# Two of the seven half-size products of each FFN chunk issued as 512-column passes over an operand's high and low parts

## The chip, the cores and the metric

One core of one Trainium2 chip. The metric is the device time of one execution in microseconds (us). Before the change it was 820.54 us, the median of 3 runs (820.32 to 820.89). All other times below come from one profiled execution.

## The reference

One encoder layer on 512 positions of width 1024: a feed-forward network (FFN), a mixer (Fourier part and attention), a second FFN, a last norm.

```
def swiglu(h, w_gate, w_up, w_down):
    return (jax.nn.silu(h @ w_gate) * (h @ w_up)) @ w_down
...
        x = x + 0.5 * swiglu(rms_norm(x, ffn1_norm), ffn1_w_gate, ffn1_w_up, ffn1_w_down)
        ...
        x = x + 0.5 * swiglu(rms_norm(x, ffn2_norm), ffn2_w_gate, ffn2_w_up, ffn2_w_down)
    return rms_norm(x, final_norm)
```

`w_gate` and `w_up` are 1024 x 2752, `w_down` is 2752 x 1024. The 2752 hidden units are 21 chunks of 128 and a tail of 64. The change is in how the gate and up products of most chunks are made, in both FFNs.

## The kernel before

**Precision.** [...] ScalarE (ACT) makes a high part with a copy that rounds, VectorE (DVE) the low part with a subtraction (`lows`, L127 and L128).

**Seven products.** With the positions in two halves of 256 and the depth in two halves of 512, the gate and up products of a chunk are one 2 x 2 block product. It is done by seven products in place of eight (a Strassen-Winograd scheme). The operand's seven combinations are made once per FFN by `operands` (L333) and kept as high and low parts in the tile `rt`: `[P, 7, 2, KH, HALF]`, that is combination, high or low, depth block (KH = 4), 256 positions. The weights' combinations are made for every chunk by `prepare` (L366): the DMAs of the raw weights are issued by SP, DVE adds and subtracts (`combine`, L394), ACT rounds (L379, L388), DVE subtracts (L128), and the parts lie in slots of the tile `ring`. The products are named by their weights: a11, a12, s1, s2, s4, s3, a22.

**One chunk.** `seven` (L407) runs over the chunks of a group. For a chunk, `multiply` (L413) writes a product as 12 passes of 256 columns (4 depth blocks by 3 passes) into half of a 512-column PSUM bank. `step` (L431) gives their order and what reads the banks:

| step | product | bank | then |
|---|---|---|---|
| 0 | a11 | r, opened | ACT copies r to p1 (L428) |
| 1 | a12 | p2, opened | DVE: g right half = p2 + p1 (L441) |
| 9 of the chunk ahead | a22 | its r | ACT copies r to u right half (L464), DVE u = g * u, ACT and DVE split it into `at` |
| 3 | s1 | q, opened | ACT copies q to p5 (L428) |
| 4 | s2 | r, added to | ACT copies r to u2 (L428) |
| 5 | s4 | q, added to | DVE: g left half = q + u2 (L451), ACT silu over g (L452) |
| 6 | s3 | r, added to | ACT copies r to u left half (L456), DVE adds p5 (L457) |

A product that adds to a bank can start only when the copy of what the bank held is done: s4 waits for the copy to p5, s2 for that to p1, s3 for that to u2. Pieces of `prepare` for the next chunk stand between the steps.

**Groups.** After the chunks of a group `down` (L485) makes the eight 128-row blocks of the down product for that group: 512-column passes (L184, tile `dn`) that read `at` and weights in `ring`. The operands of a 512-column pass are read and written in the order 4 x 32 x 4 (`turned`, L177), and what they read as operand begins four elements into its tile (NEAR, and FRONT + LOWER, L28, L116 and L292); `rt` has no such shift. In all 35 chunks go through `seven` (17 in the first FFN, 18 in the second, 5 or 6 in each group). At the start of each group one 256-column pass is cut in 64 and 192 columns (CUT, L41 and L160).

**Order.** PE and SP run in the order of the code (L121). For ACT, DVE and GpSimd (POOL) the tile framework's scheduler sets the order when the program is built, so a change of one instruction can move others on these engines.

Of the kernel before, what the change touches and what calls it, by code (L numbers as in the profile page):

```python
# [6 lines left out]
F32 = mybir.dt.float32  # L7
F32R = mybir.dt.float32r
# [24 lines left out]
GROUPS2 = ((0, "t", 1), range(2, 8), range(8, 14), range(14, 21))  # L33
PLACES = 7
HALF = S // 2
USES = "a11", "a12", "s1", "s2", "s4", "s3", "a22"
PIECES = (0, 2, 2, 0, 2, 1, 1)
KH = KD // 2
# [48 lines left out]
def encoder(ctx, tc, A, out):  # L87
# [19 lines left out]
    def bank(name):  # L107
        return pp.tile([P, S], F32, tag="bank", name=name)
# [173 lines left out]
    def ffn(norm, after, wgu, wd, wdt, groups, opening, closing):  # L282
# [6 lines left out]
        with tc.tile_pool(name=f"act{n_}", bufs=1) as ap, tc.tile_pool(name=f"sums{n_}", bufs=2) as sp:  # L289
            room(ap, 128)  # L290
            acts = ap.tile([P, PLACES * 2 * S + ROOM], F32R, name=f"at{n_}")
            at = acts[:, FRONT + LOWER : FRONT + LOWER + PLACES * 2 * S].rearrange("p (n a b) -> p n a b", a=2, b=S)  # L292
            rt = ap.tile([P, 7, 2, KH, HALF], F32R, name=f"rt{n_}")
            wt, raws = [], {}
            free, where = list(range(PLACES)), {}

# [36 lines left out]
            def operands(rp, i0, i1):  # L333
                for i in range(i0, i1):
# [72 lines left out]
            def seven(js, done):  # L407
# [4 lines left out]

                def multiply(ps, wn, on, w, first):  # L413

                    (whi, wlo), (mhi, mlo) = w[wn], (part[on][:, i] for i in range(2))
                    for i in range(KH):
                        ks = slice(i * P, (i + 1) * P)
                        for o, (a, b) in enumerate(((whi, mhi), (whi, mlo), (wlo, mhi))):
                            for t in parts_of(next(count)):
                                nc.tensor.matmul(  # L420
                                    ps[:, t], a[:, ks], b[:, i, t], start=first and i == 0 and o == 0,
                                    stop=i == KH - 1 and o == 2, skip_group_check=not first,
                                )
                    give(*w.get((wn, "slots"), ()))

                def kept(ps, n, j):
                    t = sp.tile([P, HALF], F32, tag=n, name=f"{n}{n_}_{j}")
                    nc.scalar.copy(t, ps)  # L428
                    return t

                def step(j, w, n):  # L431
                    b = banks.setdefault(j, {})
                    if n == 0:
                        b["r"] = bank(f"r{n_}_{j}")[:, :HALF]
                        multiply(b["r"], "a11", "b11", w, True)
                        b["p1"] = kept(b["r"], "p1", j)
                    elif n == 1:
                        ps = bank(f"p2{n_}_{j}")[:, :HALF]
                        multiply(ps, "a12", "b21", w, True)
                        b["g"] = tp.tile([P, S], F32, tag="g", name=f"g{n_}_{j}")  # L440
                        nc.vector.tensor_tensor(out=b["g"][:, HALF:], in0=ps, in1=b["p1"], op=ALU.add)  # L441
                    elif n == 3:
                        b["q"] = bank(f"q{n_}_{j}")[:, :HALF]
                        multiply(b["q"], "s1", "t1", w, True)
                        b["p5"] = kept(b["q"], "p5", j)
                    elif n == 4:
                        multiply(b["r"], "s2", "t2", w, False)
                        b["u2"] = kept(b["r"], "u2", j)
                    elif n == 5:
                        multiply(b["q"], "s4", "b22", w, False)  # L450
                        nc.vector.tensor_tensor(out=b["g"][:, :HALF], in0=b["q"], in1=b["u2"], op=ALU.add)  # L451
                        nc.scalar.activation(b["g"], b["g"], AF.Silu)  # L452
                    elif n == 6:
                        multiply(b["r"], "s3", "t3", w, False)
                        b["u"] = tp.tile([P, S], F32, tag="u", name=f"u{n_}_{j}")
                        nc.scalar.copy(b["u"][:, :HALF], b["r"])  # L456
                        nc.vector.tensor_tensor(  # L457
                            out=b["u"][:, :HALF], in0=b["u"][:, :HALF], in1=b["p5"], op=ALU.add
                        )
                    elif n == 9:  # L460
                        multiply(b["r"], "a22", "t4", w, False)
                        u, i = b["u"], place(j)
                        h, l = at[:, i, 0], at[:, i, 1]
                        nc.scalar.copy(u[:, HALF:], b["r"])  # L464
# [1071 lines left out]
```

## Time and profile before

| | |
|---|---|
| median of 3 runs | 820.54 us |
| the profiled execution, whole | 820.94 us |
| its span, first to last instruction | 818.9 us |
| PE busy | 812.4 us (99%), 5362 matmuls |
| DVE busy | 637.5 us (78%), 1003 instructions |
| ACT busy | 483.1 us (59%), 810 instructions |
| DMA | 89.97 MB, mean 110 GB/s |
| granted TensorE clock | full in all 40 slices |

A matmul's duration in the profile is that of one pass from start to end (276 ns for 256 columns, 380 for 512). Passes overlap, so what a pass costs on PE is the distance from its start to the next pass's start. It is read from two rows of the timeline: the difference of their starts, divided by the passes between them. The same holds for DVE, whose instructions overlap a little.

### The profile page before, as it was taken

To read this page: it belongs to the slowest core of one execution; us is meant where nothing else is said; L and a number is where in the kernel's file an instruction comes from. 1 tells how busy PE (TensorE), PEld (TensorE's weight loads), DVE (VectorE), ACT (ScalarE), POOL (GpSimd) and SP (SyncE) were. 2 spreads that over 40 slices of the span, in tenths; PEclk is the share of its full clock that TensorE was granted. 3 is DMA by queue.
4 is the path that set the end of the run, shared out by engine and by line. 5 is a ranking of instruction groups with operands and counts; after the bars stand their busy time and mean duration, and the time that the engine had idled before them with its cause. 6 is when DMAs were issued, how large, how long until landed. Compare 5 with 4: busy or idle time off the path is not lost.

```text
span 818.9 us, 13611 instructions
## 1 busy us (share of the span) xinstructions
PE 812.4 (99%) x5362; PEld 746.1 (91%) x5362; DVE 637.5 (78%) x1003; ACT 483.1 (59%) x810; POOL 29.3 (4%) x31
## 2 busy tenths in 40 slices
PE   9999999999999999999999999999999999999997
PEld 7889999899989998889998888899989999899987
DVE  7898896479856847799998578999945896479574
ACT  7763674257523735699998448456632673257462
POOL 0110000000000000221000001100000000000001
PEclk9999999999999999999999999999999999999999
DMA  7664322333141223342101234542232322322222
GB/s 258 174 145 179 124 93 77 124 104 142 59 151 71 90 70 116 129 147 66 65 26 52 77 112 127 123 176 108 94 122 114 127 100 69 132 104 97 69 78 103
DMA packets 31568, 89.97 MB, mean 110 GB/s; under 512 B 3728, under 2 KB 9232, under 8 KB 31504
## 3 DMA queue, kind: packets, MB, share of 16 engines
q1 hardware_dynamic: 27776, 82.61, 29.1%
q0 software_dynamic: 3008, 5.51, 3.7%
q10 hardware_dynamic: 720, 0.98, 0.3%
q8 instruction: 42, 0.69, 0.3%
q14 instruction: 22, 0.18, 0.1%
HBM read 84.24 MB, written 2.10 MB: 105 GB/s over the span
## 4 chain that ended last, share of the span: by engine, by line
PE 95%; DVE 2%; ACT 1%; POOL 1%; issue 1%; DMA 0%; POOLq 0%; DVEq 0%; ACTq 0%
PE dn L184 25%; PE r L420 23%; PE q L420 12%; PE gu L184 8%; PE mix L184 6%; PE p L420 6%; PE gu L709 3%; PE mix L1203 2%; PE mix L1169 2%; PE mix L1007 1%; PE mix L1008 1%; PE mix L1009 1%; PE mix L1066 1%; PE mix L1143 1%; PE mix L1144 1%
## 5 line engine op out<-in xcount | busy, mean ns | idle before, releaser
L420 PE MATMUL r<-rt,ring 128*128 128x256 f32 x1686 | 209.2, 276 | 0.0
L184 PE MATMUL dn<-at,ring 128*128 128x512 f32 x900 | 202.5, 380 | 0.0
L420 PEld LDWEIGHTS r<-rt,ring 128*128 128x128 f32 x1686 | 200.3, 188 | 0.8
L184 PEld LDWEIGHTS dn<-at,ring 128*128 128x128 f32 x900 | 168.0, 188 | 28.3
L420 PE MATMUL q<-rt,ring 128*128 128x256 f32 x840 | 106.6, 276 | 0.0
L128 DVE TENSOR_TENSOR ring<-s,ring 128x1024 fp32r<-128x1024 f32 x70 | 85.5, 1221 | 23.8 <-ACT ring L379 20.8
L420 PEld LDWEIGHTS q<-rt,ring 128*128 128x128 f32 x840 | 100.4, 188 | 0.0
L544 DVE SCALAR_TENSOR_TENSOR gx<-dn,gx 128x512 f32<-128x512 f32 x61 | 41.9, 688 | 67.1 <-PE dn L184 67.1
L379 ACT CAST ring<-s 128x1024 fp32r<-128x1024 f32 x70 | 73.5, 1050 | 28.3 <-PE p L420 13.7
L170 ACT CAST ring<-raw_dn 128x768 fp32r<-128x768 f32 (+3 forms) x58 | 45.3, 784 | 72.8 <-PE dn L184 61.9
L128 DVE TENSOR_TENSOR ring<-raw_dn,ring 128x768 fp32r<-128x768 f32 (+3 forms) x58 | 51.5, 892 | 5.7 <-PE r L420 4.4
L420 PE MATMUL p<-rt,ring 128*128 128x256 f32 x420 | 53.3, 276 | 0.0
L128 DVE TENSOR_TENSOR ring<-raw_g,ring 128x1024 fp32r<-128x1024 f32 x35 | 42.7, 1220 | 11.7 <-PE p L420 10.2
L420 PEld LDWEIGHTS p<-rt,ring 128*128 128x128 f32 x420 | 50.2, 188 | 0.0
L184 PE MATMUL gu<-ring 128*128 128x512 f32 x216 | 48.9, 381 | 0.0
L379 ACT CAST ring<-raw_g 128x1024 fp32r<-128x1024 f32 x35 | 36.8, 1051 | 17.2 <-DMA raw_g<-in_wgu 11.5
L184 PEld LDWEIGHTS gu<-ring 128*128 128x128 f32 x216 | 40.4, 188 | 6.9
L428 ACT COPY p<-r 128x256 f32<-128x256 f32 x35 | 12.9, 369 | 44.9 <-PE r L420 44.6
L452 ACT ACTIVATE g<-g 128x512 f32<-128x512 f32 x35 | 22.2, 633 | 23.9 <-DVE g L451 23.6
L388 ACT CAST ring<-raw_u 128x512 fp32r<-128x512 f32 x35 | 21.8, 624 | 16.0 <-PE q L420 15.7
L184 PE MATMUL mix<-near,ring 128*128 128x512 f32 x120 | 28.8, 381 | 0.0
L465 DVE TENSOR_TENSOR u<-g,u 128x512 f32<-128x512 f32 x35 | 24.0, 687 | 6.1 <-ACT u L464 6.0
(266 smaller groups left out, 1314.3 us busy)
## 6 DMA issues: line engine op xcount, KB each, us to landing
raw_g<-in_wgu SPq DMA_DIRECT2D x35, 512.0 KB, 3.8
raw_u<-in_wgu SPq DMA_DIRECT2D x35, 512.0 KB, 4.3
raw_dn<-in_wd SPq DMA_DIRECT2D x40, 384.0 KB, 3.1
raw_gu<-in_wgu SPq DMA_DIRECT2D x12, 512.0 KB, 3.7
raw_o<-in_wo SPq DMA_DIRECT2D x8, 512.0 KB, 3.5
raw_dn<-in_wd SPq DMA_DIRECT2D x8, 448.0 KB, 3.7
raw_wq<-in_wins SPq DMA_DIRECT2D x4, 512.0 KB, 3.5
raw_f<-in_winf SPq DMA_DIRECT2D x4, 512.0 KB, 3.5
```

The lines of the kernel that those rows point to most:

```text
L128: nc.vector.tensor_tensor(out=lo, in0=src, in1=asf(hi), op=ALU.subtract)
L170: nc.scalar.copy(hi[:, :n, :], raw[:, :n, :])
L184: nc.tensor.matmul(ps, a, b, start=first and b is mhi and a is whi, stop=last and a is wlo)
L379: nc.scalar.copy(hi, src)
L388: nc.scalar.copy(hi, src)
L420: nc.tensor.matmul(ps[:, t], a[:, ks], b[:, i, t], start=first and i == 0 and o == 0, stop=i == KH - 1 and o == 2, skip_group_check=not first,
L452: nc.scalar.activation(b["g"], b["g"], AF.Silu)
L465: nc.vector.tensor_tensor(out=u, in0=b["g"], in1=u, op=ALU.mult)
L544: nc.vector.scalar_tensor_tensor(out=x[d][:, t], in0=ps[:, t], scalar=0.5, in1=x[d][:, t], op0=ALU.mult, op1=ALU.add)
L709: nc.tensor.matmul(turned(pss[c]), w[:, k % 2, c], turned(m[k]), start=k == 0 and m is hh and w is hi, stop=k == KD - 1 and w is lo,)
L1169: nc.tensor.transpose(pts[n][:, c * P : (c + 1) * P], prob[t, b, c][:, kc * P : (kc + 1) * P], ident)
L1203: nc.tensor.matmul(turned(outs[t, b]), w, turned(p), start=kc == 0 and i == 0, stop=kc == 3 and i == 1)
```

## The change

`rt` becomes `[P, 7, KH, 2, HALF]`, so that for a depth block the 256 high columns and the 256 low ones lie side by side. The products a12 and s4 (`WIDE`) are then made of eight passes and not twelve: four passes of 512 columns, high weights by high and low operand at once, which leave two sums in the two halves of the bank, and after them four passes of 256 columns, low weights by high operand, into the left half. DVE adds the two halves: where it added one half and a tile (L441, L451), it now adds one half and the tile, and then the other half. The other five products keep their twelve passes in their order. a12 and s4 are those whose bank DVE reads; the other five, read by ACT, go through the same helpers as before.

```
-            rt = ap.tile([P, 7, 2, KH, HALF], F32R, name=f"rt{n_}")
+            rt = ap.tile([P, 7, KH, 2, HALF], F32R, name=f"rt{n_}")
...
-                        h, l = rt[:, c, 0, i], rt[:, c, 1, i]
+                        h, l = rt[:, c, i, 0], rt[:, c, i, 1]
...
-                    (whi, wlo), (mhi, mlo) = w[wn], (part[on][:, i] for i in range(2))
+                    whi, wlo = w[wn]
                     for i in range(KH):
-                        ks = slice(i * P, (i + 1) * P)
-                        for o, (a, b) in enumerate(((whi, mhi), (whi, mlo), (wlo, mhi))):
-                            for t in parts_of(next(count)):
-                                nc.tensor.matmul(
-                                    ps[:, t], a[:, ks], b[:, i, t], start=first and i == 0 and o == 0,
-                                    stop=i == KH - 1 and o == 2, skip_group_check=not first,
-                                )
+                        ks, m = slice(i * P, (i + 1) * P), part[on][:, i].rearrange("p a b -> p (a b)")
+                        start, stop = first and i == 0, i == KH - 1
+                        if wn in WIDE:
+                            nc.tensor.matmul(turned(ps), whi[:, ks], turned(m), start=start, stop=False, skip_group_check=True)
...
+                    if wn in WIDE:
+                        for i in range(KH):
+                            ks, m = slice(i * P, (i + 1) * P), part[on][:, i, 0]
+                            nc.tensor.matmul(
+                                ps[:, :HALF], wlo[:, ks], m, start=False, stop=i == KH - 1, skip_group_check=True
+                            )
...
+                def added(out, ps, other, n):
+                    nc.vector.tensor_tensor(out=out, in0=ps[:, :HALF], in1=other, op=ALU.add)
+                    if n in WIDE:
+                        nc.vector.tensor_tensor(out=out, in0=ps[:, HALF:], in1=out, op=ALU.add)
...
-                        nc.vector.tensor_tensor(out=b["g"][:, HALF:], in0=ps, in1=b["p1"], op=ALU.add)
+                        added(b["g"][:, HALF:], ps, b["p1"], "a12")
...
-                        nc.vector.tensor_tensor(out=b["g"][:, :HALF], in0=b["q"], in1=b["u2"], op=ALU.add)
+                        added(b["g"][:, :HALF], b["q"], b["u2"], "s4")
```

PE has 5070 matmuls in the program in place of 5350, DVE 70 additions more. SP and POOL keep their order. What moves is shown at three places.

PE, in the chunk 8 of the first FFN, before; `r_8`, `p_8` and `q_8` are the banks of this chunk, `r_7` that of the chunk ahead.

```order
L420 MATMUL r_8_1185<-rt_129,ring 128x256 x12
L420 MATMUL p_8_1200<-rt_129,ring 128x256 x12
L420 MATMUL r_7_1063<-rt_129,ring 128x256 x12
L420 MATMUL q_8_1237<-rt_129,ring 128x256 x12
L420 MATMUL r_8_1185<-rt_129,ring 128x256 x12
```

These are a11, a12, a22 of the chunk ahead, s1 and s2, twelve passes each.

The same place on PE with the change, from the last passes of a11 to the first of a22; the passes with high weights stand at L425 and those with low weights at L430.

```order
L425 MATMUL r_8_1161<-rt_129,ring 128x256 x2
L430 MATMUL r_8_1161<-rt_129,ring 128x256
L421 MATMUL p_8_1176<-rt_129,ring 128x4x32x4 x4
L436 MATMUL p_8_1176<-rt_129,ring 128x256 x4
L425 MATMUL r_7_1045<-rt_129,ring 128x256 x2
L430 MATMUL r_7_1045<-rt_129,ring 128x256
```

The twelve passes into `p_8` are four of 512 columns and four of 256, and PE goes from 256 columns to 512 and back at each such product.

DVE, at the end of the first run of `seven` in the first FFN, before: chunk 9 is the last of that run, `raw_dn_0_1` the down weights that PE needs first behind it, `s_0_10` and `raw_g_10` belong to the first chunk of the next group.

```order
L128 TENSOR_TENSOR ring<-raw_g_10_1468,ring 128x1024
L441 TENSOR_TENSOR g_9_1329<-p_9_1316,p_9_1314 128x256
L394 TENSOR_TENSOR s_0_10_1473<-raw_g_10_1468,s_0_10_1472 128x512
L128 TENSOR_TENSOR ring<-s_0_10_1472,ring 128x1024
L465 TENSOR_TENSOR u_8_1296<-g_8_1213,u_8_1296 128x512
L128 TENSOR_TENSOR ring<-raw_u_10_1469,ring 128x512
L128 TENSOR_TENSOR ring<-raw_dn_0_1_1406,ring 128x768
L451 TENSOR_TENSOR g_9_1329<-q_9_1347,u_9_1374 128x256
L128 TENSOR_TENSOR at_128<-u_8_1296,at_128 128x512
```

The low part of the down weights stands behind one addition of this chunk (L441).

The same place on DVE with the change, where L442 is the first addition of a wide product and L444 the second.

```order
L129 TENSOR_TENSOR ring<-raw_g_10_1432,ring 128x1024
L442 TENSOR_TENSOR g_9_1295<-p_9_1286,p_9_1272 128x256
L395 TENSOR_TENSOR s_0_10_1437<-raw_g_10_1432,raw_u_10_1433 128x512
L395 TENSOR_TENSOR s_0_10_1437<-raw_g_10_1432,s_0_10_1436 128x512
L493 TENSOR_TENSOR u_8_1266<-g_8_1185,u_8_1266 128x512
L129 TENSOR_TENSOR ring<-s_0_10_1436,ring 128x1024
L444 TENSOR_TENSOR g_9_1295<-p_9_1286,g_9_1295 128x256
L129 TENSOR_TENSOR ring<-raw_u_10_1433,ring 128x512
L129 TENSOR_TENSOR ring<-raw_dn_0_1_1370,ring 128x768
L442 TENSOR_TENSOR g_9_1295<-q_9_1314,u_9_1341 128x256
L129 TENSOR_TENSOR at_128<-u_8_1266,at_128 128x512
```

The low part of the down weights now stands behind the second addition of chunk 9 too, and behind both second additions of chunk 8.

ACT, in the chunks 8 and 9, before: L452 is the silu of a chunk, `p_8` with `q_8` the copy to p5 for which s4 waits, `u_8` with `r_8` the copies out of the bank r.

```order
L428 COPY p_8_1250<-q_8_1237 128x256
L428 COPY u_8_1264<-r_8_1185 128x256
L379 CAST ring<-s_0_9_1184 128x1024
L466 CAST at_128<-u_7_1174 128x512
L452 ACTIVATE g_8_1213<-g_8_1213 128x512
L456 COPY u_8_1296<-r_8_1185 128x256
L379 CAST ring<-raw_g_10_1468 128x1024
L428 COPY p_9_1314<-r_9_1301 128x256
L379 CAST ring<-s_0_10_1472 128x1024
L464 COPY u_8_1296<-r_8_1185 128x256
```

The silu stands ahead of three copies and casts of the same chunk.

The same place on ACT with the change, where L476 is the silu and L447 all copies but that of step 6 (L486).

```order
L447 COPY p_8_1211<-q_8_1210 128x256
L447 COPY u_8_1237<-r_8_1161 128x256
L380 CAST ring<-s_0_9_1160 128x1024
L494 CAST at_128<-u_7_1150 128x512
L486 COPY u_8_1266<-r_8_1161 128x256
L380 CAST ring<-raw_g_10_1432 128x1024
L447 COPY p_9_1272<-r_9_1271 128x256
L476 ACTIVATE g_8_1185<-g_8_1185 128x512
L447 COPY u_8_1266<-r_8_1161 128x256
L380 CAST ring<-s_0_10_1436 128x1024
```

The silu, which now waits for the second addition, has moved behind three instructions, into the next chunk, closer to the copies that come after it there; it does so in most chunks.

More of the change, by code (lines that the diff above doesn't have):

```diff
@@ L35 @@
 HALF = S // 2
+WIDE = ('a12', 's4')
 USES = "a11", "a12", "s1", "s2", "s4", "s3", "a22"
@@ L424, in multiply @@
-                    give(*w.get((wn, "slots"), ()))
[L426 to L429, printed above, removed]
+                        ks, m = slice(i * P, (i + 1) * P), part[on][:, i].rearrange("p a b -> p (a b)")
+                        start, stop = first and i == 0, i == KH - 1
+                        if wn in WIDE:
+                            nc.tensor.matmul(turned(ps), whi[:, ks], turned(m), start=start, stop=False, skip_group_check=True)
+                        else:
+                            for o in range(2):
+                                for t in parts_of(next(count)):
+                                    nc.tensor.matmul(
+                                        ps[:, t], whi[:, ks], m[:, o * HALF :][:, t], start=start and o == 0, stop=False,
+                                        skip_group_check=True,
+                                    )
```

39 lines of the change are left out of this document (28 added, 11 removed).

## The prediction

> **What bounds the kernel now.** I read the page's busy times and chain first, then busy time by stretch, then the timeline of one chunk.
>
> ```profile
> PE 812.4 (99%) x5362; PEld 746.1 (91%) x5362; DVE 637.5 (78%) x1003; ACT 483.1 (59%) x810; POOL 29.3 (4%) x31
> PE 95%; DVE 2%; ACT 1%; POOL 1%; issue 1%; DMA 0%; POOLq 0%; DVEq 0%; ACTq 0%
> PE dn L184 25%; PE r L420 23%; PE q L420 12%; PE gu L184 8%; PE mix L184 6%; PE p L420 6%; PE gu L709 3%; PE mix L1203 2%; PE mix L1169 2%; PE mix L1007 1%; PE mix L1008 1%; PE mix L1009 1%; PE mix L1066 1%; PE mix L1143 1%; PE mix L1144 1%
> ```
>
> PE is 95% of the chain that ends last, and 41% of the span is L420, the line that changes. A nanosecond less of PE there is a nanosecond less in all, as long as nothing else comes last. The two stretches of seven products that follow, one ordinary and one with the busiest VectorE, show who could (us; then PE, PEld, DVE, ACT and POOL busy).
>
> ```profile
> 74.00:130.00 56.00, 56.00 (x495) 56.00 (x494) 49.85 (x73) 35.50 (x63) 0.00 (x0) 1.00 0.29 101
> 538.20:594.00 55.80, 55.80 (x494) 55.80 (x493) 52.69 (x79) 35.27 (x62) 0.00 (x0) 1.00 0.31 112
> ```
>
> PE has no gap in either, at the full granted clock (1.00). VectorE is busy 89% and 94% of the time: the change hands work to the second busiest engine.
>
> **The passes.** The end of a run of `seven` on PE, each row starting where its engine gets to it:
>
> ```profile
> 121.73 1.52 PE L420 MATMUL p<-rt,ring 128*128 128x256 f32 x12
> 123.09 1.52 PE L420 MATMUL r<-rt,ring 128*128 128x256 f32 x12
> ...
> 127.17 1.52 PE L420 MATMUL q<-rt,ring 128*128 128x256 f32 x12
> ...
> 129.89 4.12 PE L184 MATMUL dn<-at,ring 128*128 128x512 f32 x18
> 133.85 1.53 PE L420 MATMUL r<-rt,ring 128*128 128x256 f32 x12
> 135.21 27.88 PE L184 MATMUL dn<-at,ring 128*128 128x512 f32 x126
> ```
>
> Twelve 256-column passes take 123.09 - 121.73 = 1.36 us, 113.3 ns each. Eighteen 512-column passes take 133.85 - 129.89 = 3.96 us, 220 ns each. So one wide pass is 2 x 113.3 - 220 = 6.7 ns cheaper than the two it replaces. A wide product is 4 x 220 + 4 x 113.3 = 1333 ns where it was 1360: **26.7 ns less**. Two products in 35 chunks are 70 of them: **-1.87 us**. That is the whole gain that the trace has to give: no row that I read shows a 512-column pass cheaper than 220 ns. The 220 are taken from the `dn` passes because they write and read in the same 4 x 32 x 4 order as the new ones, and there are many of them:
>
> ```profile
> L420 PE MATMUL r<-rt,ring 128*128 128x256 f32 x1686 | 209.2, 276 | 0.0
> L184 PE MATMUL dn<-at,ring 128*128 128x512 f32 x900 | 202.5, 380 | 0.0
> ```
>
> Busy time over count is 225 ns for the second row (with the ends of its stretches), so they all run so.
>
> The Trainium skill, "PSUM — Partial Sum Buffer", Specifications (TRN2), speaks against this order: it says that any access pattern that isn't contiguous slows matmuls significantly. By it the wide passes would cost more than two halves. The `dn` rows don't bear that out: 220 ns for 512 columns in the broken order is less per column than 113.3 for 256 contiguous ones. The skill's "TensorE: Matmul & The Clock Gate", Back-to-back issue gap, gives N / 2.4 + 2.5 ns for a pass; by that fixed part a wide product would save 4 x 2.5 = 10 ns, in all 0.7 us. The rows say 6.7 ns of fixed part, and the measurement decides.
>
> **Changing widths.** Before, PE goes from 256 columns to 512 and back once or twice a group; now at every wide product. Each first pass behind such a change, from the groups of short windows around 133.85 and 135.21 (mean ns is the last but one number):
>
> ```profile
> L420 PE MATMUL r<-rt,ring 128*128 128x256 f32 x1 | 0.3, 279 | 0.0
> ...
> L184 PE MATMUL dn<-at,ring 128*128 128x512 f32 x1 | 0.4, 384 | 0.0
> ```
>
> They are 3 and 4 ns longer than the means of their groups above (276 and 380). I take these: 7 ns x 70 = **+0.49 us**. The bounds: nothing, and what the mixer's 256-column passes show behind a 512-column one:
>
> ```profile
> 410.10 0.38 PE L1144 MATMUL mix<-ks,near 128*128 128x512 f32 x1
> 410.32 0.28 PE L1007 MATMUL mix<-ring 128*128 128x256 f32 x1
> ...
> 411.26 0.28 PE L1009 MATMUL mix<-ring 128*128 128x256 f32 x1
> ...
> 412.62 0.28 PE L1009 MATMUL mix<-ring 128*128 128x256 f32 x1
> ```
>
> From 410.32 to 411.26 are 8 passes at 117.5 ns, from 411.26 to 412.62 are 12 at 113.3. A stream needs some passes to fall into step, here at 8 x 4.2 = 34 ns, which for 70 products would be 2.4 us. I stay with 7 ns, since those rows read the operands `rt` and `at` themselves.
>
> **VectorE's 70 additions.** Three rows of VectorE near the end of the same run:
>
> ```profile
> 115.57 0.42 DVE L441 TENSOR_TENSOR g<-p,p 128x256 f32<-128x256 f32 x1
> 115.90 1.22 DVE L128 TENSOR_TENSOR ring<-raw_g,ring 128x1024 fp32r<-128x1024 f32 x1
> ...
> 128.00 0.95 DVE L128 TENSOR_TENSOR ring<-raw_dn,ring 128x768 fp32r<-128x768 f32 x1
> ```
>
> An addition of this form moves the next start by 0.33 us. A run of 6 chunks gets 12 more, 4.0 us: 53.9 of 55.7 us in the ordinary stretch, where PE's own work hides them; 56.7 of 55.5 in the busiest, where about 1.2 us has to go on behind its end. PE feels lateness only where a result has little time in hand. The nearest is the low part of the first down weights: done at 128.95, and needed by the third `dn` pass at 129.89 + 2 x 0.22 = 130.33, 1.38 us in hand. Ahead of it VectorE now makes three second additions more in chunks 8 and 9 (1.0 us), and PE arrives 12 x 0.027 = 0.3 us earlier: 0.1 us is left. The second place is ScalarE's copy of q to p5, on which s4 waits:
>
> ```profile
> 126.47 0.36 ACT L428 COPY p<-q 128x256 f32<-128x256 f32 x1
> ```
>
> It ends at 126.83 and s4 starts at 127.17: 0.34 us in hand, and much the same in each chunk. ScalarE stands in line behind VectorE at the silu, which now needs the second addition:
>
> ```profile
> ACT g L452 <- DVE g L451: 23.6, 17, 1.9
> ```
>
> It waited there 23.6 us in 17 of 35 chunks, up to 1.9 us. The scheduler has put the silu (0.5 us from start to start) some instructions later, closer to the next chunk's copies; ScalarE's idle time (37% in these stretches) is the cover, but in a chunk where it has none, the copy to p5 is late by some tenths and s4, and all of PE behind it, with it. I take 0.1 us in each of some five places: **+0.5 us**. The bounds are nothing (every lateness hidden) and 3 us: 1.2 us for the busiest stretch, and 0.3 us in each of the six runs.
>
> **What costs nothing.** `rt` is as large as before, its parts are written by instructions of the same shapes while the first group's PE work covers them, and SP and POOL keep their order. The low part is needed one pass earlier in a wide product, but `rt` is complete long before. The seven-product banks are no more than before, 3 a chunk.
>
> **The sum.** -1.87 + 0.49 + 0.5 = -0.88 us. The profiled execution took 820.94 (span 818.9 and 2.0 around it), so 820.06; the median of the runs is 0.4 below that execution, so **819.7 us**.
>
> **Rivals.**
> 1. *All is hidden.* No cost at the changes of width, no waiting: 820.54 - 1.87 = 818.7. For it: the 12 x 113.3 that follow 18 x 512 at 133.85 still take 1.36 us in all. Against it: the 0.34 us in hand. 0.2.
> 2. *The wide passes run in a slower step* (slower than before). A stream of 512-column passes has a second gait:
>
> ```profile
> 331.30 5.44 PE L184 MATMUL mix<-ring 128*128 128x512 f32 x24
> 336.58 0.60 PE L1286 MATMUL mix<-ident,acc 128*128 128x128 f32 x4
> ...
> 338.70 5.14 PE L184 MATMUL mix<-ring 128*128 128x512 f32 x21
> 343.68 0.60 PE L943 MATMUL mix<-ident,kw 128*128 128x128 f32 x4
> ```
>
> 24 passes in 5.28 us are 220 ns; 21 passes of the same line and tiles, behind some small matmuls, in 4.98 us are 237 ns. What a pass reads while the next weights come in seems to matter, and here `rt` lies otherwise to the weights than the operands of any 512-column pass so far (front part: no shift of four elements). At 237 ns the 280 wide passes cost 280 x 17 = 4.76 us more: 819.66 + 4.76 = 824.4. It decides from 226.7 ns on, where the wide pass gains nothing; with the other terms the kernel is over 0.2% slower from about 229. Against it: 900 `dn` passes at 220. The skill's rule on patterns that aren't contiguous points the same way. 0.2.
> 3. *VectorE falls behind.* The additions come late, silu and p5 with them, and s4 waits in most chunks: +3 us in place of +0.5, 822.2, half of it just inside no change and half outside. For it: 94% busy in one stretch. Against it: most of VectorE's results have more in hand. The low part of `raw_g` above ends at 117.12; the next chunk's a11, for which it is made, begins 12 passes into this row, at 120.37:
>
> ```profile
> 119.01 2.88 PE L420 MATMUL r<-rt,ring 128*128 128x256 f32 x24
> ```
>
> That is over 3 us, more than the 1.2 us by which VectorE is late. 0.15.
>
> That the change doesn't do what it says is excluded by the order: 280 passes are gone.
>
> **Chances.** 0.2% is 1.64 us, about what a measurement of this kernel can tell from no change. My forecast has 0.45 and lies inside it, as does half of rival 3: same 0.52. Rival 1 ends at -1.87, just outside: faster 0.2. Rival 2 and the other half of 3: slower 0.28. The range goes from rival 1 to rival 2, 818.6 to 824.4. The likeliest case alone is 819 to 820.6.
>
> **What will show it.** In the profile after: L421 with 280 passes of 512 columns, and from the start of the four to the start of L436's first 0.88 us (rival 2: 0.92 and more); L436's four to the next product's start 0.453 us; a run of twelve behind them still 1.36. Rows of idle PE before L421 `q` with the copy of q as releaser would be the third term, and before the third `dn` pass of a group the down weights. VectorE should be busy some 23 to 29 us more in all. I am wrong if wide passes need over 224 ns, or if PE shows waits of over 1 us in a run of `seven`.

## The result, and the profile after

The changed kernel took 827.31 us (median of 4 runs, 827.14 to 827.76) beside 820.71 for the kernel before (4 runs, 820.32 to 821.59): a ratio of 1.0078, 95% interval 1.0066 to 1.009. It is slower by 6.6 us, where 819.7 was predicted; the time lies outside the range. The profiled execution took 827.76 us with a span of 824.7.

From the page of the changed kernel: busy time, the chain by engine and by line, and the groups of the seven products. The columns behind the bar are busy us, mean ns of one, and idle time ahead.

```profile
PE 818.1 (99%) x5082; PEld 741.1 (90%) x5082; DVE 661.4 (80%) x1073; ACT 483.9 (59%) x810; POOL 29.3 (4%) x31
...
PE 92%; DVE 4%; ACT 1%; DMA 1%; issue 1%; POOL 0%; POOLq 0%; DVEq 0%; ACTq 0%; SPq 0%
PE dn L185 25%; PE r L425 16%; PE mix L185 8%; PE r L430 8%; PE q L425 4%; PE p L421 4%; PE q L421 4%; PE gu L185 4%; PE gu L737 3%; PE q L430 2%; PE p L436 2%; PE q L436 2%; PE mix L1231 2%; PE mix L1197 2%; PE mix L1035 1%; PE mix L1036 1%
...
L425 PE MATMUL r<-rt,ring 128*128 128x256 f32 x1126 | 199.8, 278 | 0.0
...
L430 PE MATMUL r<-rt,ring 128*128 128x256 f32 x560 | 156.0, 279 | 0.0
...
L421 PE MATMUL p<-rt,ring 128*128 128x512 f32 x140 | 37.5, 388 | 0.0
L421 PE MATMUL q<-rt,ring 128*128 128x512 f32 x140 | 37.3, 386 | 0.0
```

The 280 wide passes are there. PE, the engine of the matmuls (TensorE), has 280 of them less, and it is busy 5.7 us *more* (818.1 against 812.4). Two signs point at PE's own pace: the wide passes' means are 388 and 386 ns where the `dn` passes have 380, and the narrow passes, which the change leaves as they were, have risen from 276 to 278 and 279. (A narrow pass has 256 columns, a wide one 512; a narrow product has, for each depth block, two passes with high weights and one with low, a wide one first its four wide passes and then four narrow ones with low weights.)

Where PE waited, in the whole profile after (us in total, times, longest):

```profile
PE busy L682 <- PEq L1547: 0.8, 1, 0.8
PE gu L737 <- ACT ring L723: 0.3, 1, 0.3
```

Both lie at the kernel's start. One more wait, in the seven products, is not in this list, since the records of PE's passes overlap it. It stands in a single chunk of the third run:

```profile
288.01 0.38 ACT L447 COPY p<-q 128x256 f32<-128x256 f32 x1
288.20 0.28 PE L430 MATMUL r<-rt,ring 128*128 128x256 f32 x1
...
288.45 1.18 PE L421 MATMUL q<-rt,ring 128*128 128x512 f32 x4
...
289.47 0.63 PE L436 MATMUL q<-rt,ring 128*128 128x256 f32 x4
```

s4 begins 0.06 us after the end of ScalarE's copy of q to p5 (288.39), 0.25 us behind the start of the last pass of s2, where 0.12 is usual. s2 and s4 take 0.25 us too long between them. In the other 34 chunks that copy ends 0.26 us or more before s4 starts, and PE does not wait. Busy time in the two stretches of before (the first lasts 0.6 us longer now; us, then PE, PEld, DVE, ACT, POOL):

```profile
74.00:130.60 56.60, 56.60 (x443) 54.76 (x443) 52.88 (x84) 35.76 (x63) 0.00 (x0) 1.00 0.30 97
538.20:594.00 55.80, 55.80 (x430) 53.72 (x429) 54.53 (x88) 34.34 (x59) 0.00 (x0) 1.00 0.36 123
```

VectorE is busy 93% and 98% of these, the granted clock is 1.00, PE has no gap. So it is the passes themselves that take longer. One chunk and what follows it, on PE; a row is a group of like passes with its start, and the difference of two starts is what PE needed:

```profile
92.98 1.07 PE L421 MATMUL p<-rt,ring 128*128 128x512 f32 x4
93.89 0.63 PE L436 MATMUL p<-rt,ring 128*128 128x256 f32 x4
94.36 0.40 PE L425 MATMUL r<-rt,ring 128*128 128x256 f32 x2
...
95.77 0.40 PE L425 MATMUL q<-rt,ring 128*128 128x256 f32 x2
...
97.18 0.40 PE L425 MATMUL r<-rt,ring 128*128 128x256 f32 x2
...
98.59 1.06 PE L421 MATMUL q<-rt,ring 128*128 128x512 f32 x4
99.50 0.63 PE L436 MATMUL q<-rt,ring 128*128 128x256 f32 x4
99.96 0.39 PE L425 MATMUL r<-rt,ring 128*128 128x256 f32 x2
...
102.68 0.39 PE L421 MATMUL p<-rt,ring 128*128 128x512 f32 x1
```

Read it from the top. a12's four wide passes take 93.89 - 92.98 = 0.91 us, its four low ones 0.47. Then come a22, s1 and s2, twelve narrow passes each, which the change did not touch: 95.77 - 94.36 = 1.41, 1.41 and 1.41 us. Then s4, 0.91 and 0.46, and behind it s3 and a11 together 102.68 - 99.96 = 2.72, that is 1.36 each as before. **The narrow passes have two paces**, 1.36 / 12 = 113.3 ns (below: the quick step) and 1.413 / 12 = 117.8 ns (the slow step), and at each wide product PE goes over from one to the other.

From the start times of all passes in the trace, per product, from its first pass to the first of what follows (mean of 35, us):

| | a11 | a12 | a22 | s1 | s2 | s4 | s3 | sum of all 35 chunks |
|---|---|---|---|---|---|---|---|---|
| before | 1.382 | 1.360 | 1.361 | 1.360 | 1.360 | 1.360 | 1.360 | 334.0 |
| after | 1.382 | 1.379 | 1.405 | 1.413 | 1.417 | 1.371 | 1.360 | 340.5 |

(a11 holds the cut pass at the head of each of the six runs.) The sum is 6.5 us longer: this is the whole loss, and 0.25 us of it is the wait above (in s2 and s4). Below, "the sum" is this one; what lies outside it took 484.2 us after, 484.9 before, and 484 to 487 in all profiles here, so the sum tells more than one execution's time.

A longer block of wide passes elsewhere does no such thing. The end of the same group, where 18 `dn` passes stand between a11 and the last a22:

```profile
130.44 4.12 PE L185 MATMUL dn<-at,ring 128*128 128x512 f32 x18
134.41 0.39 PE L425 MATMUL r<-rt,ring 128*128 128x256 f32 x2
...
135.77 4.56 PE L185 MATMUL dn<-at,ring 128*128 128x512 f32 x20
```

18 passes in 3.97 us are 220 ns, and the product behind them takes 1.36.

### The profile page after: what moved, and what is told of

It is laid out like the page before. It is cut to its first block, busy times and chain, and to the rows that moved or that the text cites. A ratio compares the mean times of both kernels' runs of the same rounds, so it can differ in the third digit from the quotient of the medians.

```text
span 824.7 us, 13090 instructions
## 1 busy us (share of the span) xinstructions
PE 818.1 (99%) x5082; PEld 741.1 (90%) x5082; DVE 661.4 (80%) x1073; ACT 483.9 (59%) x810; POOL 29.3 (4%) x31
## 4 chain that ended last, share of the span: by engine, by line
PE 92%; DVE 4%; ACT 1%; DMA 1%; issue 1%; POOL 0%; POOLq 0%; DVEq 0%; ACTq 0%; SPq 0%
PE dn L185 25%; PE r L425 16%; PE mix L185 8%; PE r L430 8%; PE q L425 4%; PE p L421 4%; PE q L421 4%; PE gu L185 4%; PE gu L737 3%; PE q L430 2%; PE p L436 2%; PE q L436 2%; PE mix L1231 2%; PE mix L1197 2%; PE mix L1035 1%; PE mix L1036 1%
## 5 line engine op out<-in xcount | busy, mean ns | idle before, releaser
L425 PE MATMUL r<-rt,ring 128*128 128x256 f32 x1126 | 199.8, 278 | 0.0
L425 PEld LDWEIGHTS r<-rt,ring 128*128 128x128 f32 x1126 | 172.2, 189 | 0.8
L430 PE MATMUL r<-rt,ring 128*128 128x256 f32 x560 | 156.0, 279 | 0.0
L430 PEld LDWEIGHTS r<-rt,ring 128*128 128x128 f32 x560 | 105.1, 188 | 0.0
L425 PE MATMUL q<-rt,ring 128*128 128x256 f32 x280 | 51.0, 281 | 0.0
L447 ACT COPY u<-r 128x256 f32<-128x256 f32 x70 | 26.1, 373 | 38.2 <-PE r L430 37.3
L425 PEld LDWEIGHTS q<-rt,ring 128*128 128x128 f32 x280 | 43.2, 190 | 0.0
L447 ACT COPY p<-r 128x256 f32<-128x256 f32 x35 | 12.9, 368 | 46.6 <-PE r L430 45.9
L430 PE MATMUL q<-rt,ring 128*128 128x256 f32 x140 | 39.3, 281 | 0.0
L421 PE MATMUL p<-rt,ring 128*128 128x512 f32 x140 | 37.5, 388 | 0.0
L421 PE MATMUL q<-rt,ring 128*128 128x512 f32 x140 | 37.3, 386 | 0.0
```

The lines of the kernel that those rows point to most:

```text
L421: nc.tensor.matmul(turned(ps), whi[:, ks], turned(m), start=start, stop=False, skip_group_check=True)
L425: nc.tensor.matmul(ps[:, t], whi[:, ks], m[:, o * HALF :][:, t], start=start and o == 0, stop=False, skip_group_check=True,)
L430: nc.tensor.matmul(ps[:, :HALF], wlo[:, ks], m[:, :HALF], start=False, stop=stop, skip_group_check=True)
L447: nc.scalar.copy(out, ps[:, HALF:] if wide else ps[:, :HALF])
```

## The experiments

The theories, as they are named in the expectations. **G**: each wide product switches the step of all later passes, from quick to slow or back. **P**: certain products are slow for their own operands or places. **V**: VectorE's second additions (or what waits for them) are the cost. **L**: the new layout of `rt` and the helpers cost something by themselves. All kernels start from the changed one. "Before" beside them was 821.04 us for 1 to 4, 821.21 for 5, 7, 8 and 9, 821.25 for 6, 10, 14 and 15, and 821.01 for 11, 12 and 13.

**1. No wide product.**

```
-WIDE = ('a12', 's4')
+WIDE = ()
```

> The changed kernel with no product made wide: the new layout of rt, the new helpers, twelve 256-column passes per product again. Theory G (the gait of PE's passes: a wide product leaves the stream of 256-column passes in a slower step, 117.7 ns in place of 113.3, until the next wide product): no wide product, so all products at 1.36 us and the time of before, 820.7. Rival L (the new layout of rt is what makes 256-column passes slower): products at 1.40 to 1.41 us, 826 or more. Rival V (VectorE's 70 additions): 820.7 too.

820.91 us, ratio 0.9996 (0.9987 to 1.0006); the sum is 334.0 and each product takes 1.360. L falls: the layout and the helpers cost nothing.

**2 and 3. One wide product a chunk.** `WIDE = ('s4',)` and `WIDE = ('a12',)`.

> Only s4 is wide. Theory G in its switching form (each wide product turns a fast step into a slow one and a slow one into a fast one): there is one wide product a chunk, so the 72 other passes of a chunk are fast in one chunk and slow in the next: 35 x (11 + 0.5 x 72 x 4.4) ns = 5.9 us more than before, 826.6, with products at 1.36 and 1.41 us in turn. Rival P (what follows depends on the product: after s4 always fast, after a12 always slow): 35 x 11 ns = 0.4 us more, 821.1. Rival V (the additions cost): half of the loss of 6.6 us, 824.

> Only a12 is wide. Theory G in its switching form: as with s4 alone, fast and slow chunks in turn, 35 x (19 + 158) ns = 6.2 us more, 826.9. Rival P (after a12 always slow): all 72 other passes of each chunk slow, 35 x (19 + 317) ns = 11.8 us more, 832.5. Rival V: 824.

With s4 alone 826.45 us, ratio 1.0069 (1.0054 to 1.0084), sum 340.0; with a12 alone 828.72, ratio 1.0089 (1.0073 to 1.0105), sum 339.9. Half as many wide products cost about as much as all of them. In both, the narrow products of one chunk run at 1.360 us and those of the next at 1.413 to 1.414, in turn, all through a run: one switch a chunk. The wide product takes 1.379 us when it is entered in the quick step and 1.367 or 1.368 in the slow one. G's sums are met, and P's times (821.1 and 832.5) are not; with a12 alone the time is 1.8 us above G's 826.9. (There one of the four runs took 826.14, and the profiled one has 2 us more outside the sum; that part is not explained.)

**4. Without the second additions.** The lines `if n in WIDE: ... in0=ps[:, HALF:], in1=out` of `added` are left out, so that the right half of the bank is never added.

> Both products wide on PE, but VectorE's second additions are left out, so that the product with the low part of the operand is missing from a12 and s4. Theory G: PE's passes are what they are, 827.3, with a22, s1 and s2 at 1.40 to 1.42 us. Rival V (VectorE's 70 additions, by waiting or by traffic in the memories): back to 820.7 or below, at most to 818.7.

827.95 us, ratio 1.0088 (1.0073 to 1.0103), sum 340.4. Without VectorE's 70 additions nothing is gained, and s4 still waits for the copy to p5 in one chunk (0.15 us, at 766 us). V falls.

**5. Two wide products next to each other: a12 and a22.** `WIDE = ('a12', 'a22')`.

> a12 and a22 are the wide products, in place of a12 and s4: on PE they stand next to each other (a12 of a chunk, then a22 of the chunk before). Theory G (each wide product switches the step of all passes behind it from 113.3 to 117.7 ns or back): the second switches back at once what the first has switched, so that the five narrow products between two pairs all run at 1.360 us; the pair costs 1.379 + 1.368 us where two narrow ones take 2.720. In 35 chunks that is +0.9 us: 821.9 us. Rival W (a wide product leaves whatever follows slow until PE gets to other work): 5 of 7 products at 1.414 us, +9 us, 830. Rival A (the passes of a22 slow for their own operand): 826 to 828.

831.53 us, ratio 1.0116 (1.0098 to 1.0133), sum 344.0: the time of the rival W, and nearly 10 us from what I expected. The trace on PE shows G at work all the same:

```profile
83.49 1.06 PE L421 MATMUL p<-rt,ring 128*128 128x512 f32 x4
84.39 0.63 PE L436 MATMUL p<-rt,ring 128*128 128x256 f32 x4
84.86 1.07 PE L421 MATMUL r<-rt,ring 128*128 128x512 f32 x4
85.77 0.63 PE L436 MATMUL r<-rt,ring 128*128 128x256 f32 x4
86.24 0.40 PE L425 MATMUL q<-rt,ring 128*128 128x256 f32 x2
...
87.65 0.40 PE L425 MATMUL r<-rt,ring 128*128 128x256 f32 x2
```

a12 takes 84.86 - 83.49 = 1.37 (so it was entered in the slow step), a22 1.38 (entered in the quick one), and s1 behind them 1.41: two switches that cancel, but from slow to slow. The fault was in my start. In the first chunk of a run there is no a22 yet (it belongs to the chunk ahead), so the first a12 stands alone, makes the step slow, and every pair after it hands the slow step on. I tested that with a pair that is complete in every chunk.

**6. s4 and s3.** `WIDE = ('s4', 's3')`.

> s4 and s3 are the wide products. They stand next to each other in every chunk, the first of a run too (a12 and a22 did not: there the first a12 stood alone, and left the whole run slow). Theory G (each wide product of the broken order switches the step): s4 is entered at 113.3 and takes 1.379, s3 is entered at 117.7, takes 1.368 and switches back; the five narrow products stay at 1.360 us in all chunks: 334.0 + 35 x (1.379 + 1.368 - 2.720) = 334.9 us, 821.9 us in all. Rival W (wide products leave slow passes behind, and only cuts or other work bring the quick ones back): five products at 1.414, 831.

823.70 us, ratio 1.0023 (1.0014 to 1.0032), sum 335.7:

```profile
97.37 0.39 PE L425 MATMUL r<-rt,ring 128*128 128x256 f32 x2
...
98.73 1.07 PE L421 MATMUL q<-rt,ring 128*128 128x512 f32 x4
99.64 0.63 PE L436 MATMUL q<-rt,ring 128*128 128x256 f32 x4
100.11 1.06 PE L421 MATMUL r<-rt,ring 128*128 128x512 f32 x4
101.01 0.63 PE L436 MATMUL r<-rt,ring 128*128 128x256 f32 x4
101.47 0.39 PE L425 MATMUL r<-rt,ring 128*128 128x256 f32 x2
...
102.83 0.39 PE L425 MATMUL p<-rt,ring 128*128 128x256 f32 x2
```

s2 takes 98.73 - 97.37 = 1.36, the pair 1.38 + 1.36, a11 behind it 1.36: the second has switched back. That holds in every chunk up to 760 us. There s2 and s4 take 0.4 us too long between them, and the products of the next chunk run in the slow step; two last a22 behind down passes are slow as well. The list of waits names no releaser, but the copy to p5 ends at 760.79 and s4 starts at 760.84: it is the wait that the changed kernel has at 288. Without these the sum would be near the 334.9 expected. W falls, and G's switching is borne out: as many wide products as in the changed kernel, and over half of its loss gone.

**7. The start of `rt`.** The operand begins four elements (16 bytes) later, as `at` does.

```
-            rt = ap.tile([P, 7, KH, 2, HALF], F32R, name=f"rt{n_}")
+            rts = ap.tile([P, 7 * KH * S + ROOM], F32R, name=f"rt{n_}")
+            rt = rts[:, NEAR : NEAR + 7 * KH * S].rearrange("p (n k a b) -> p n k a b", k=KH, a=2, b=HALF)
```

> The operand rt begins four elements (16 bytes) later, as at does, which the 220 ns passes of the down weights read; the rest is the changed kernel. Theory S (the step depends on where a pass reads against where the next weights lie, and this shift is what the dn passes have and the wide ones lack): wide passes at 220 ns, nothing is switched: the seven products take 334.0 - 1.9 = 332.1 us, 819.1 us in all. The 256-column passes, which never ran at this shift, could be slower for it: at 117.7 ns for all 2,374 of them the kernel would take 829.5. Rival W2 (what switches is the change of width itself, wherever the operand lies): 827.4 as the changed kernel, a12 1.379 and three slow products behind it.

835.65 us, ratio 1.0167 (1.0148 to 1.0186), sum 347.6. S falls as a cure: the wide passes take 225.5 ns on average and not 220. It is right in its premise that the place of the operand counts, for the narrow passes above all. a22, s1 and s2 in one chunk:

```profile
95.13 0.41 PE L426 MATMUL r<-rt,ring 128*128 128x256 f32 x2
...
96.57 0.40 PE L426 MATMUL q<-rt,ring 128*128 128x256 f32 x2
...
97.99 0.41 PE L426 MATMUL r<-rt,ring 128*128 128x256 f32 x2
...
99.43 0.39 PE L422 MATMUL q<-rt,ring 128*128 128x512 f32 x1
```

1.44, 1.42 and 1.44 us, where the changed kernel has 1.41 for the same instructions; s3 and a11, which are quick there (1.36), take 1.43, and the last a22 of a run, behind `dn` passes, takes 1.44 for 1.36. The step changes from pass to pass (the last section has the series). The tile is also 64 elements longer, and narrow products alone were not run at this place.

**8 to 11. What of a wide product switches.** Experiment 8 puts the wide passes in plain order (`turned` taken from L421), 9 puts each low pass right behind its wide pass, 10 makes two wide, two low, two wide, two low, and 11 has only the first two depth blocks wide and the others in narrow passes.

> The wide passes write and read their 512 columns in plain order, not 4 x 32 x 4. Theory O (the broken order switches the step): wide passes at 220 ns, narrow ones 1.360 us, 819.1 us. Theory G with any order (the 512 columns switch, not their order): 827.4 us as the changed kernel, slow products between a12 and s4. If plain order is slower in itself (such passes elsewhere in the kernel, of other operands, take 230 to 236 ns): 280 x 6 ns = 1.7 us more than the changed kernel, 829.

> In a wide product each 512-column pass is followed at once by its pass with the low weights: eight changes of width in a product, not two. Theory G in the form that each block of 512 columns switches the step once: four switches in a product cancel, so that it leaves the step as it found it, and the products between a12 and s4 run at 1.360 us; the wide ones at 1.36 to 1.40 us: 334.0 to 335.4 us for the seven products, 821 to 822.5 us. Rival I (the product switches once, however its passes are arranged): 827 us. Rival C (each change of width costs its own few ns and nothing is switched): a12 and s4 alone slower, by four times what two changes cost.

> The wide products a12 and s4 are made as 2 wide passes, their 2 passes with the low weights, 2 wide, 2 low. Theory G with one switch for each block of wide passes: two switches in a product, so the narrow products all run at 1.360 us; the wide ones at 1.37 to 1.39: 334.9 to 336 us for the seven products, 822 to 823 us. Rival N (it takes four passes in a row to switch; shorter blocks only disturb what is near): the same time, but passes inside the product that show no 117.7 ns step between the blocks. Rival I (the sum of the wide passes counts): 827.

> In a12 and s4 only the first two of the four row blocks are wide passes; the other two are done in narrow passes, and the two low-weight passes of the wide ones come last: 2 wide and 8 narrow. Theory B (any block of wide passes switches once): slow products between a12 and s4 as in the changed kernel, about 340.5 us for the seven products, 827 us. Theory F (it takes four passes; two leave the step as it was, as one did and twice two did): narrow products all at 1.360, the two products at some 1.375: 335 us, 822 us.

| | median us | ratio (95%) | sum us | wide products us |
|---|---|---|---|---|
| 8, plain order | 823.63 | 1.0028 (1.0016 to 1.0039) | 336.0 | 1.387, 1.390 |
| 9, each low pass behind its wide one | 823.95 | 1.0031 (1.002 to 1.0042) | 337.0 | 1.384, 1.389 |
| 10, two and two | 823.62 | 1.0032 (1.0021 to 1.0043) | 336.0 | 1.386, 1.389 |
| 11, only two wide | 822.88 | 1.0021 (1.0012 to 1.003) | 336.0 | 1.387, 1.389 |

None of the four switches, and in all of them wide products are slower than narrow ones. (The second number, s4, holds one wait of about 0.1 us for the copy to p5, in 9 two.) The time from each pass to the next in one chunk, ns, worked out from the start times in the trace (a star is a wide pass; behind the bar the first passes of the next product):

```
after, a12    *228 *233 *229 *220  119  115  118  117 | 118  118  118  117
after, s4     *229 *222 *224 *227  117  119  116  114 | 113  113  114  113
8,  a12       *226 *236 *231 *236  118  113  114  113 | 113  114  113  113
9,  a12       *227  117 *224  123 *224  122 *224  123 | 117  122  116  114
10, a12       *228 *232  116  118 *228 *226  122  116 | 114  114  112  114
11, a12       *227 *233  116  119  121  116  114  114  113  113 | 114  113
12, s4 and s3 *227 *234 *229 *220 *224 *227 *233 *229  117  117  119  116
```

The wide passes of `rt` do not run at one pace: in the broken order they go through 227, 233, 229, 220, 224, 227, 233, 229, and where the row stops decides in which step the narrow passes behind it run. Four from the quick step end it where the slow step begins; one or two lead back to the quick step within some passes. In plain order they take 226 to 236 and lead back always. The Trainium skill, "PSUM — Partial Sum Buffer", Specifications (TRN2), says that any access that isn't contiguous slows matmuls significantly. Here the contiguous wide passes are the slower ones (929 ns for four, against 902 to 910).

**12. Eight wide passes in a row**, those of s4 and of s3, and their eight low ones behind them.

```
-                    elif n == 5:
-                        multiply(b["q"], "s4", "b22", w, False)
+                    elif n == 6:
+                        for k in ({"low": False}, {"wide": False}):
+                            multiply(b["q"], "s4", "b22", w, False, **k)
+                            multiply(b["r"], "s3", "t3", w, False, **k)
```

> s4 and s3 are the wide products, and their eight wide passes stand in a row, their eight low-weight passes behind them. Theory B (a block of wide passes switches once, however long): one switch in a chunk, so the five narrow products run at 1.360 us in one chunk and 1.414 in the next, as with s4 alone: about 339 us for the seven products, 826 us. Theory F (each four wide passes shift the step once, so eight are back where they began): the narrow products all at 1.360, the pair 0.91 + 0.90 + 0.93 = 2.74 us: 334.9 us, 822 us. Either way the fifth to eighth pass show whether a longer row comes down to 220 ns.

824.09 us, ratio 1.0037 (1.0026 to 1.0047), sum 337.1. Behind the eight, the narrow products take 1.360 us in all chunks but one: F's side, it is the number of passes that counts, not the block. The one chunk follows a wait of 0.3 us ahead of the eight, at 761 us, for the copy of q. (Another wait, 0.7 us for the copy of r at 199 us, falls between the fourth and the fifth pass and leaves the quick step behind it.) In 6, too, a wait stood ahead of the one pair of wide products that led to the slow step. So a pause of PE may take part in where the row stops; these are few cases, and no run was made to test it. The row above shows that a longer one does not come down to 220 ns either: its mean is 228.

**13. A cut pass behind a12.** The second pass of the product that follows a12 is cut in 64 and 192 columns, as one pass at the start of each group is already.

```
-                                for t in parts_of(next(count)):
+                                for t in parts_of(CUT[0] if cut and i == 0 and o == 1 else next(count)):
```

> The changed kernel with one cut pass more (64 and 192 columns for 256) in the product that follows a12, as before's schedule has at the start of each run. A cut costs 130 ns (1.490 us for such a product against 1.360). Theory R (a cut sets the quick step, whatever went before): quick products behind it up to s4, which is now entered quick, takes 1.379 and leaves s3 and the next a11 slow: 1.414 + 1.369 + 3 x 1.360 + 0.130 + 1.379 + 1.414 = 9.79 us a chunk, 343 us, 830 us. Theory T (a cut switches the step, as a block of wide passes does): the same products slow or quick in alternate chunks, much the same time: the trace tells, by s4 entered at 113 or 118 ns. If a cut does nothing to the step: 340.5 + 35 x 0.13 = 345 us, 832 us.

830.99 us, ratio 1.0124 (1.0106 to 1.0142), sum 343.0, as theory R had it:

```profile
93.63 1.06 PE L421 MATMUL p<-rt,ring 128*128 128x512 f32 x4
94.53 0.63 PE L436 MATMUL p<-rt,ring 128*128 128x256 f32 x4
95.00 0.48 PE L425 MATMUL r<-rt,ring 128*128 128x256 f32 x3
...
96.48 0.39 PE L425 MATMUL q<-rt,ring 128*128 128x256 f32 x2
...
97.84 0.39 PE L425 MATMUL r<-rt,ring 128*128 128x256 f32 x2
...
99.20 0.39 PE L421 MATMUL q<-rt,ring 128*128 128x512 f32 x1
```

In the first chunk of a run a12 leaves the slow step, and the cut product behind it (s1 there, 1.500 us) ends in the quick one. In the later chunks a12 is entered slow (95.00 - 93.63 = 1.37) and leaves the quick step, and the cut leaves it quick: a22 with it takes 1.48, s1 and s2 1.36. s4 is entered quick in every chunk and, in all but one, makes s3 and a11 slow. (In that one, at 678 us, s4 waited for the copy to p5, and s3 and a11 behind it are quick.) So a cut sets and does not switch, T falls, and each run begins in the quick step behind the cut at its head. A cut costs 130 ns where it could save 162 here (3 products by 54 ns), and s3 and a11, now slow, cost another 107.

**14 and 15. All passes in the broken order**, with `rt` shifted as in 7, and with `rt` in its place.

```
-    ps[:, t], whi[:, ks], m[:, o * HALF :][:, t], start=start and o == 0, stop=False,
+    turned(ps[:, t]), whi[:, ks], turned(m[:, o * HALF :][:, t]), start=start and o == 0, stop=False,
```

> The operand rt lies four elements later, and all passes of the seven products, narrow ones too (4 x 16 x 4), are in the broken order: everything that the 220 ns passes of the down weights have. Theory S2 (position and order together set the step, and a stream in which neither changes runs quickly): wide passes 220, narrow 113.3, 819.1 us. Rival (the shift slows 256-column passes whatever their order, as it did in plain order, 1.423 to 1.437 us for a product): 834 to 836.

> All passes of the seven products are in the broken order (narrow ones 4 x 16 x 4), and rt lies where the changed kernel has it. Theory O2 (what switches the step is the change from plain to broken order and back): nothing switches, narrow 1.360 and wide 1.333 us, 819.1 us. Theory G (the four 512-column passes switch, whatever stands around them): a12 1.379 and slow products behind it, 827.4. If the broken order is slow for 256 columns: more than that.

With the shift 824.28 us, ratio 1.003 (1.0017 to 1.0043), sum 337.2; in place 823.02, ratio 1.0017 (1.0007 to 1.0026). Neither forecast is met, and each is half right. With the shift some chunks do reach the price that the change needs, four wide passes at 221, 220, 220 and 220 ns and 1.336 us for the product; but the narrow ones then take 1.37 to 1.38, and up to 1.43 in the first two chunks of a run. In place, one chunk:

```profile
93.13 1.05 PE L421 MATMUL p<-rt,ring 128*128 128x512 f32 x4
94.03 0.61 PE L436 MATMUL p<-rt,ring 128*128 128x256 f32 x4
94.48 0.39 PE L425 MATMUL r<-rt,ring 128*128 128x256 f32 x2
...
95.85 0.39 PE L425 MATMUL q<-rt,ring 128*128 128x256 f32 x2
```

Nothing switches, a12 takes 0.90 + 0.45 = 1.35 us, 0.01 less than a narrow product did before, and the narrow one 1.37, 0.01 more; there are five of those to two wide ones. No arrangement that was run is quicker than the kernel before.

## Why the prediction was wrong

- **The gain by count (-1.87 us): mis-sized, nothing is left of it.** It took the wide pass at 220 ns, from 900 `dn` passes. Those of `rt` take 226.9 (63.5 us for 280, from the start times): +1.9 us, which alone eats the gain (0.1 of it is the wait of s4). The step at fault is "because they write and read in the same 4 x 32 x 4 order": the order is not enough. The place of the operand counts as well (7: moved by 16 bytes, the narrow products that were quick take 5% longer), and so does the order of the passes around (15: 224 ns beside narrow passes in the broken order). A longer row does not help (12: 228 ns). The prediction's own sign of being wrong, wide passes that need over 224 ns, came.
- **"Changing widths" (+0.49 us, at most 2.4): the step that failed.** I took what a change costs to be the few ns by which its first pass is longer, and at most some passes until the stream "falls into step". There is no one step to fall into. The change leaves the stream in the other step, and it stays there for 36 passes, until the next wide product. The four low-weight passes took 116.9 ns where I had 113.3, +1.0 us, and a22, s1 and s2 took 148.2 us where they had 142.8: **+5.4 us**, in instructions that were not edited (0.13 us of it is the wait, in s2). -1.87 + 1.9 + 1.0 + 5.4 = +6.4 accounts for the measured 6.5. The mixer rows quoted in the prediction showed both paces, 117.5 and 113.3, in a stream that came back by itself; that the passes of `rt` would come back too had no row behind it.
- **VectorE's additions (+0.5 us, at most 3): the path was right, the size half, the cause not shown.** I took 0.1 us in each of some five places; the trace has one, 0.25 us, and it is the one named, s4 behind the copy of q to p5. Such a wait is there without the second additions as well (4: 0.15 us), and leaving them out gains nothing; why the copy comes late was not tested. VectorE has 23.9 us more to do, as worked out (661.4 against 637.5), and is busy 98% of one stretch. PE's slower pace is not what hides that: in 11 PE keeps the quick step with both second additions made, every narrow product but the cut ones takes 1.360 (1.364 at most), and s4 waits in one chunk, by 0.1 us. Rival 3, waits in most chunks, falls.
- **What costs nothing: right** (1).
- **Rival 2** had the nearest reason, that `rt` lies otherwise to the weights (not shown as it stands: at the start that `at` has, the wide passes took 225.5, in 7), and named the point at which the wide pass gains nothing, 226.7 ns; they took 226.9. Its price of 237 ns was too high for the wide passes, and it was silent on the narrow ones, which made 5.4 of the 6.5 us. The evidence I used for rival 1, a quick product behind 18 `dn` passes, still stands in the profile after; it did not speak for four passes of another operand.
- **What would show it**: "a run of twelve behind them still 1.36" was the right row to name; it reads 1.41 behind a12.

What stays open is the mechanism below this: why one stream has two steps, and why four wide passes take it from one to the other. The runs show that the place of the operand, the order of its columns, the number of wide passes in a row and a cut pass decide it; nothing in the profile shows how.

## What to carry to other kernels

Where one engine is the bound and its instructions run in step, price an edit by the pace of what stands *behind* it too, with the same operands, places and count as the edit has; a pace taken from other tiles is an estimate, and its range has to hold the other pace for all passes up to the next thing that resets it. When untouched instructions show a higher mean in the new profile, compare start times group by group before looking for a wait. And saving instructions at 6.7 ns each is worth less than the difference of two steps (4.4 ns) over the many that remain.

## What the hardware showed that I had not expected

- A stream of like matmuls has two steady steps at the same granted clock of 1.00 and with no wait: 113.3 and 117.8 ns for 256 columns with a new weight load each.
- Four passes of 512 columns of `rt` in the order 4 x 32 x 4 change one into the other, in both directions, and cost 1.379 or 1.368 us with their four narrow ones by the step they start from; one, two and eight do not, nor do four in plain order.
- A pass cut in 64 and 192 columns sets the quick step within about six passes (141, 120, 116, 117, 114, 113 ns behind it).
- 16 bytes in the start of the moving operand turn 113.3 ns into a series that repeats about every eight passes, 120, 124, 121, 119, 114, 119, 119, 117 ns, and a product that took 1.360 us into one of 1.42 to 1.44.
- 512 columns of `rt` in the order 4 x 32 x 4 took 227 to 228 ns on average in blocks of four and eight (220 in the `dn` passes), in plain order 232; 256 columns in such an order 114.4 (15), in plain order 113.3.
